# Sending the last 128 row sums as four transposed rows of 128 B instead of within 128 pieces of 64 B

## The chip, the cores and the metric

The kernel runs on one core of a Trainium2 chip. The metric is device time in microseconds (us), lower is better. Every ratio below is between runs in the fast state, on the same chip and in the same rounds. The profile's span, from the first to the last instruction, is some 1.8 us shorter than the device time of the same run; small differences are read best from the profiles. Two limits: each profile is one execution, and profiles of different experiments come from different chips; and the four runs that issue many stores one by one were executed once, so their state is unknown.

Engines: VectorE (DVE in the profile), ScalarE (ACT), SyncE (SP, whose queue "SPq" issues nearly all transfers), and 16 DMA engines that move the data.

## The reference

```python
batch, seq, dim = 32, 512, 1024
# x: float32, (batch, seq, dim); multiplier: 0.5
def reference(x, multiplier):
    return (np.sum(x, axis=-1) * multiplier).astype(np.float32)
```

That is 16,384 rows of 1024 floats (67.1 MB) in, and 16,384 sums (64 KB) out.

## The kernel before

Each of the 128 partitions owns rows that lie next to each other in memory, and takes them in blocks of 16. Seven blocks come from the first 14,336 rows, the eighth from the last 2,048. VectorE sums whole blocks; from the middle of the seventh block on, VectorE and ScalarE share the rows, and those of the eighth arrive in ever smaller pieces, so that little work is left when the last byte is in. The very last piece is columns 576 to 1023 of one row per partition.

```python
x_rows = x_flat[0 : P * own, :].rearrange("(p c) d -> p c d", p=P)
x_last = x_flat[P * own : N, :].rearrange("(p c) d -> p c d", p=P)
out_rows = out_flat[0 : P * own].rearrange("(p c) -> p c", p=P)
out_last = out_flat[P * own : N].rearrange("(p c) -> p c", p=P)
...
for lo, hi in [(0, 8), (8, 13), (13, 15)]:               # rows of the last block
    loads.append(nc.sync.dma_start(out=t[:, lo:hi, :], in_=x_last[:, lo:hi, :]))
for lo, hi in ((0, cut), (cut, D)):                      # cut = 576: the last row in two
    loads.append(nc.sync.dma_start(out=t[:, B - 1, lo:hi], in_=x_last[:, B - 1, lo:hi]))
early = nc.sync.dma_start(out=out_rows, in_=res[:, 0:own])      # 56 KB of results
for r in range(B - 1):
    ...                                                  # ScalarE or VectorE, a row each
dve_span(t, B - 1, 0, cut, part)
final = dve_span(t, B - 1, cut, D, res[:, rows - 1 : rows], start=part)
seen = nop_after(nc.sync, loads[-8:] + acts[-1:], [])
store = nc.sync.dma_start(out=out_last, in_=res[:, own:])       # 8 KB, 64 B a partition
nop_after(nc.sync, [early, final], [store])
```

`out_last` gives each partition 16 neighbouring results, so the last store is 128 pieces of 64 B, and it must wait for the very last sum.

Of the kernel before, what the change touches and what calls it, by code (L numbers as in the profile page):

```python
# [1 line left out]

# [4 lines left out]


@with_exitstack
def kernel(  # L10
    ctx: ExitStack,
    tc: tile.TileContext,
    x: bass.AP,
    multiplier: float,
    out: bass.AP,
):










    nc = tc.nc
    P = nc.NUM_PARTITIONS
    fp32 = mybir.dt.float32
    ADD = mybir.AluOpType.add  # L30

    x_flat = x.flatten_outer_dims()
    N, D = x_flat.shape
    rows = N // P
    out_flat = out.rearrange("b s -> (b s)")
    mul = float(multiplier)

    B = 16
    n_blocks = rows // B
    assert N == P * rows and rows == n_blocks * B  # L40
    own = rows - B
    x_rows = x_flat[0 : P * own, :].rearrange("(p c) d -> p c d", p=P)
    x_last = x_flat[P * own : N, :].rearrange("(p c) d -> p c d", p=P)
    out_rows = out_flat[0 : P * own].rearrange("(p c) -> p c", p=P)
    out_last = out_flat[P * own : N].rearrange("(p c) -> p c", p=P)

    x_pool = ctx.enter_context(tc.tile_pool(name="x", bufs=3))
    res_pool = ctx.enter_context(tc.tile_pool(name="res", bufs=1))
    sums = res_pool.tile([P, rows], fp32, name="sums")
    res = res_pool.tile([P, rows], fp32, name="res")  # L50
    part = res_pool.tile([P, 1], fp32, name="part")

    SYNC = mybir.DependencyInfo(mybir.DependencyClass.Sync, mybir.DependencyReason.DATA)
    ORDER = mybir.DependencyInfo(
        mybir.DependencyClass.NoSync, mybir.DependencyReason.SCHED_ONLY
    )

    def nop_after(engine, waits_for, follows):
        i = engine.nop()
        for w in waits_for:  # L60
            tc.add_manual_dep(i.ins, w.ins.name, SYNC, reason="end seen here")
        for f in follows:
            tc.add_manual_dep(i.ins, f.ins.name, ORDER, reason="in this order")
        return i

    loads = []
    acts = []

    def act_row(t, r, col):
        acts.append(nc.scalar.activation(  # L70
            out=t[:, r, :],
            in_=t[:, r, :],
            func=mybir.ActivationFunctionType.Copy,
            scale=mul,
            accum_out=res[:, col : col + 1],
        ))

    def dve_span(t, r, lo, hi, dst, start=0.0):
        mid = (lo + hi) // 2
        return nc.vector.tensor_tensor_reduce(  # L80
            out=t[:, r, lo:mid],
            in0=t[:, r, lo:mid],
            in1=t[:, r, mid:hi],
            scale=mul,
            scalar=start,
            op0=ADD,
            op1=ADD,
            accum_out=dst,
        )

    for b in range(n_blocks - 1):
        c0 = b * B
        t = x_pool.tile([P, B, D], fp32, name="xb")
        loads.append(nc.sync.dma_start(out=t, in_=x_rows[:, c0 : c0 + B, :]))  # L94
        h = B if b < n_blocks - 2 else B // 2
        nc.vector.reduce_sum(  # L96
            out=sums[:, c0 : c0 + h], in_=t[:, 0:h, :], axis=mybir.AxisListType.X
        )
        nc.vector.tensor_single_scalar(  # L99
            out=res[:, c0 : c0 + h],  # L100
            in_=sums[:, c0 : c0 + h],
            scalar=mul,
            op=mybir.AluOpType.mult,
        )
        for r in range(h, B):
            act_row(t, r, c0 + r)

    c0 = (n_blocks - 1) * B
    t = x_pool.tile([P, B, D], fp32, name="xb")
    cut = 576  # L110
    pieces = [(0, 8), (8, 13), (13, 15)]
    for lo, hi in pieces:
        loads.append(
            nc.sync.dma_start(  # L114
                out=t[:, lo:hi, :], in_=x_last[:, lo:hi, :]
            )
        )
    for lo, hi in ((0, cut), (cut, D)):
        loads.append(
            nc.sync.dma_start(  # L120
                out=t[:, B - 1, lo:hi], in_=x_last[:, B - 1, lo:hi]
            )
        )
    early = nc.sync.dma_start(out=out_rows, in_=res[:, 0:own])
    on_act = {4, 5, 6, 7, 11, 12, 14}
    for r in range(B - 1):
        if r in on_act:
            act_row(t, r, c0 + r)
        else:
            dve_span(t, r, 0, D, res[:, c0 + r : c0 + r + 1])  # L130
    dve_span(t, B - 1, 0, cut, part)
    final = dve_span(t, B - 1, cut, D, res[:, rows - 1 : rows], start=part)




    seen = nop_after(nc.sync, loads[-8:] + acts[-1:], [])
    store = nc.sync.dma_start(out=out_last, in_=res[:, own:])
    tc.add_manual_dep(store.ins, seen.ins.name, ORDER, reason="in this order")
    for a in acts[-len(on_act) :]:  # L140
        tc.declare_no_dep(store.ins, a.ins.name, reason="waited for by the nop in front")
    nop_after(nc.sync, [early, final], [store])

    def start_loads_at_entry(nc_):



        entry, *rest = nc_.main_func.blocks
        is_sp = lambda i: i.engine == mybir.EngineType.SP
        is_load = lambda i: type(i).__name__ == "InstDMACopy"  # L150
        for block in rest:
            body = list(block.instructions)
            own = [i for i in body if is_sp(i)]
            if not any(is_load(i) for i in own):
                continue
            lead = []
            for i in own:
                if not is_load(i) or i.sync_info.on_wait:
                    break
                lead.append(i)  # L160
            names = {i.name for i in lead}
            block.instructions = [i for i in body if i.name not in names]
            head = list(entry.instructions)
            at = next(
                k for k, i in enumerate(head) if is_sp(i) and type(i).__name__ == "InstDrain"
            )
            entry.instructions = head[:at] + lead + head[at:]
            return

    nc.at_finalize(start_loads_at_entry)  # L170


# [1 line left out]
_INS = ['x', 'multiplier']  # L174
_OUTS = [((32, 512), 'float32')]

_NUMBERS = {'multiplier': 0.5}


# [26 lines left out]
```

## Time and profile before

| | before |
|---|---|
| device time, median (lowest to highest) | 162.13 us (162.12 to 162.49) |
| span in the profile | 160.517 us |
| busy share of the DMA engines | 97.5% |
| VectorE / ScalarE busy | 119.3 us / 17.3 us |
| last accumulator out | 158.315 us |
| last store: issue; last count of its semaphore | 158.344 us; 159.765 us |

The loads fill the DMA engines until the last one has landed at 157.72; then come the last sum and the last store. I call the last 2.20 us, from the last sum's accumulator to the end of the span (160.517 - 158.315), the **tail**; it doesn't contain the small differences in when the loads end. The prediction shows its lines.

How to read a store here: the profile's bar "DMA_DIRECT2D" on SPq is the issue alone. The bytes move later, in packets on the DMA engines, and the store has landed only when every engine has counted the semaphore up. I give three times for a store, all from the start of its bar: the length of the **bar**, the start of its **first packet**, and its **last count**. The first is a line of the profile, the other two are from the trace's packet and semaphore records. ("Descriptors" in the prediction are the orders for the single pieces.)

### The profile page before, as it was taken

Reading aid. Unit: us, or ns where it says so; the run is one execution under the profiler, and the core shown is the slowest. Engines: PE = TensorE matmul, PEld = TensorE weight load, DVE = VectorE, ACT = ScalarE, POOL = GpSimd, SP = SyncE. Lnnn points to the kernel's source line nnn. Section 1 sums busy time; section 2 is a strip of 40 time slices with the busy share of each in tenths; the row PEclk is TensorE's granted clock in tenths of the full one; section 3 lists DMA queues with packets and bytes.
Section 4 is the critical chain, followed back from the end, with each engine's and each line's share of the span. In section 5 each row is a group of like instructions: output and inputs, shape, how many; then the busy total and the mean of one; then the engine's idle time right before and its main releaser. Section 6 shows DMA issues by size and latency. Waiting matters only on the chain.

```text
span 160.5 us, 138 instructions
## 1 busy us (share of the span) xinstructions
DVE 119.3 (74%) x34; ACT 17.3 (11%) x31; POOL 0.2 (0%) x4
## 2 busy tenths in 40 slices
DVE  0000059998699968999599995999959999597443
ACT  0000000000000000000000000000000000599952
POOL 0000000000000000000000000000000000000000
DMA  8996996996996996996996997997998998999991
GB/s 261 523 523 261 523 506 278 523 490 294 523 490 294 523 490 294 523 490 294 523 490 294 523 474 310 523 441 343 523 425 359 523 425 359 392 433 425 439 368 50
DMA packets 2016, 67.18 MB, mean 418 GB/s; under 512 B 480, under 2 KB 608, under 8 KB 736
## 3 DMA queue, kind: packets, MB, share of 16 engines
q1 hardware_dynamic: 2016, 67.18, 97.5%
HBM read 67.11 MB, written 0.07 MB: 418 GB/s over the span
## 4 chain that ended last, share of the span: by engine, by line
DMA 75%; DVE 22%; SPq 1%; issue 0%; DVEq 0%
DMA xb<-in_x_dram 75%; DVE sums L96 21%; SPq L114 1%; DVE xb L80 0%; SPq L120 0%; SPq L94 0%; DVE res L99 0%; DVEq L80 0%; DVEq L201 0%
## 5 line engine op out<-in xcount | busy, mean ns | idle before, releaser
L96 DVE TENSOR_REDUCE sums<-xb 128x16 f32<-128x16384 f32 (+1 forms) x7 | 112.0, 16001 | 33.6 <-DMA xb<-in_x_dram 33.6
L70 ACT ACT_TABLE_LOAD x1 | 1.3, 1283 | 138.2 <-DMA xb<-in_x_dram 138.2
L70 ACT ACTIVATE xb<-xb 128x1024 f32<-128x1024 f32 x15 | 15.7, 1045 | 2.1 <-DMA xb<-in_x_dram 2.1
L80 DVE CUSTOM_DVE_ANT_0 xb<-xb 128x512 f32<-128x512 f32 (+1 forms) x9 | 5.6, 663 | 5.0 <-DMA xb<-in_x_dram 5.0
L70 ACT ACTIVATION_READ_ACCUMULATOR xb<-xb 128x1 f32 x15 | 2.8, 187 | 0.0
L99 DVE TENSOR_SCALAR res<-sums 128x16 f32<-128x16 f32 (+1 forms) x7 | 1.2, 174 | 0.2
L80 DVE DVE_READ_ACCUMULATOR2_ANT res<- 128x1 f32 x9 | 0.7, 83 | 0.0
L80 DVE CUSTOM_DVE_ANT_0 xb<-xb,part 128x224 f32<-128x224 f32 x1 | 0.5, 452 | 0.2 <-DMA xb<-in_x_dram 0.2
L187 POOL MEMSET const-bfloat16-1.0<- 128x1 bf16 x1 | 0.1, 102 | 0.0
L187 POOL MEMSET const-uint8-127<- 128x1 uint8 x1 | 0.1, 102 | 0.0
L187 POOL MEMSET const-float32-0.0<- 128x1 f32 x1 | 0.1, 99 | 0.2 <-issue 0.2
L187 POOL MEMSET const-float32-1.0<- 128x1 f32 x1 | 0.1, 99 | 0.0
L80 DVE DVE_READ_ACCUMULATOR2_ANT part<- 128x1 f32 x1 | 0.1, 83 | 0.0
## 6 DMA issues: line engine op xcount, KB each, us to landing
xb<-in_x_dram SPq DMA_DIRECT2D x1, 4096.0 KB, 31.1
xb<-in_x_dram SPq DMA_DIRECT2D x1, 2560.0 KB, 36.9
xb<-in_x_dram SPq DMA_DIRECT2D x1, 1024.0 KB, 38.9
xb<-in_x_dram SPq DMA_DIRECT2D x1, 288.0 KB, 39.1
xb<-in_x_dram SPq DMA_DIRECT2D x1, 224.0 KB, 39.2
xb<-in_x_dram SPq DMA_DIRECT2D x7, 40.8
out_dram<-res SPq DMA_DIRECT2D x1, 56.0 KB, 10.0
out_dram<-res SPq DMA_DIRECT2D x1, 8.0 KB, 1.4
```

Of the source, the lines that this page charges most:

```text
L70: acts.append(nc.scalar.activation(out=t[:, r, :], in_=t[:, r, :], func=mybir.ActivationFunctionType.Copy, scale=mul, accum_out=res[:, col ...
L80: return nc.vector.tensor_tensor_reduce(out=t[:, r, lo:mid], in0=t[:, r, lo:mid], in1=t[:, r, mid:hi], scale=mul, scalar=start, op0=ADD, o ...
L96: nc.vector.reduce_sum(out=sums[:, c0 : c0 + h], in_=t[:, 0:h, :], axis=mybir.AxisListType.X)
L99: nc.vector.tensor_single_scalar(out=res[:, c0 : c0 + h], in_=sums[:, c0 : c0 + h], scalar=mul, op=mybir.AluOpType.mult,)
L114: nc.sync.dma_start(out=t[:, lo:hi, :], in_=x_last[:, lo:hi, :])
L187: nc = _bacc.Bacc("TRN2", target_bir_lowering=False, num_devices=1)
```

## The change

The intent is to have less at the end: rather than 128 pieces of 64 B, only four rows of 128 B should be stored after the last sum. To that end the last row of all partitions becomes the last 128 rows of x, so that its sums are 512 neighbouring bytes of the output. They are a column, one per partition. VectorE's transpose in 32x32 squares turns it into four rows, on partitions 0, 32, 64 and 96. The other 15 results of each partition leave a little earlier, from ScalarE's queue.

```diff
+    few = B - 1
+    x_next = x_flat[P * own : P * (own + few), :].rearrange("(p c) d -> p c d", p=P)
+    x_last = x_flat[P * (own + few) : N, :]
+    out_next = out_flat[P * own : P * (own + few)].rearrange("(p c) -> p c", p=P)
+    S = 32
+    out_last = out_flat[P * (own + few) : N].rearrange("(q s) -> q s", s=S)
...
+    last = res_pool.tile([P, S], fp32, name="last")
+    turned = res_pool.tile([P, S], fp32, name="turned")
+    nc.vector.memset(last, 0.0)
...
-    final = dve_span(t, B - 1, cut, D, res[:, rows - 1 : rows], start=part)
+    dve_span(t, B - 1, cut, D, last[:, 0:1], start=part)
+    final = nc.vector.transpose(out=turned, in_=last)
+    middle = nc.scalar.dma_start(out=out_next, in_=res[:, own:])
...
-    store = nc.sync.dma_start(out=out_last, in_=res[:, own:])
+    store = nc.sync.dma_start(out=out_last, in_=turned[0:P:S, :])
```

(Cut here: the loads of the last block read `x_next` and `x_last` accordingly, `res` has one column less, and the wait at the end includes `middle`.)

More of the change, by code (lines that the diff above doesn't have):

```diff
@@ L42 @@
     x_rows = x_flat[0 : P * own, :].rearrange("(p c) d -> p c d", p=P)
-    x_last = x_flat[P * own : N, :].rearrange("(p c) d -> p c d", p=P)
+    few = B - 1
+    x_next = x_flat[P * own : P * (own + few), :].rearrange("(p c) d -> p c d", p=P)
+    x_last = x_flat[P * (own + few) : N, :]
     out_rows = out_flat[0 : P * own].rearrange("(p c) -> p c", p=P)
-    out_last = out_flat[P * own : N].rearrange("(p c) -> p c", p=P)
+    out_next = out_flat[P * own : P * (own + few)].rearrange("(p c) -> p c", p=P)
+    S = 32
+    out_last = out_flat[P * (own + few) : N].rearrange("(q s) -> q s", s=S)
     x_pool = ctx.enter_context(tc.tile_pool(name="x", bufs=3))
@@ L49 @@
     sums = res_pool.tile([P, rows], fp32, name="sums")
-    res = res_pool.tile([P, rows], fp32, name="res")
+    res = res_pool.tile([P, own + few], fp32, name="res")
+    last = res_pool.tile([P, S], fp32, name="last")
+    turned = res_pool.tile([P, S], fp32, name="turned")
+    nc.vector.memset(last, 0.0)
     part = res_pool.tile([P, 1], fp32, name="part")
@@ L114 @@
             nc.sync.dma_start(
-                out=t[:, lo:hi, :], in_=x_last[:, lo:hi, :]
+                out=t[:, lo:hi, :], in_=x_next[:, lo:hi, :]
             )
@@ L120 @@
             nc.sync.dma_start(
-                out=t[:, B - 1, lo:hi], in_=x_last[:, B - 1, lo:hi]
+                out=t[:, B - 1, lo:hi], in_=x_last[:, lo:hi]
             )
@@ L131 @@
     dve_span(t, B - 1, 0, cut, part)
-    final = dve_span(t, B - 1, cut, D, res[:, rows - 1 : rows], start=part)
+    dve_span(t, B - 1, cut, D, last[:, 0:1], start=part)
+    final = nc.vector.transpose(out=turned, in_=last)
+    middle = nc.scalar.dma_start(out=out_next, in_=res[:, own:])
     seen = nop_after(nc.sync, loads[-8:] + acts[-1:], [])
-    store = nc.sync.dma_start(out=out_last, in_=res[:, own:])
+    store = nc.sync.dma_start(out=out_last, in_=turned[0:P:S, :])
     tc.add_manual_dep(store.ins, seen.ins.name, ORDER, reason="in this order")
-    for a in acts[-len(on_act) :]:
-        tc.declare_no_dep(store.ins, a.ins.name, reason="waited for by the nop in front")
-    nop_after(nc.sync, [early, final], [store])
+    nop_after(nc.sync, [early, middle, final], [store])
     def start_loads_at_entry(nc_):
```

## The prediction

> **What bounds the kernel now.** I began with the page's engine table and its chain of work that ended last, to learn whether an engine or the transfers set the end.
>
> ```profile
> span 160.5 us, 138 instructions
> DVE 119.3 (74%) x34; ACT 17.3 (11%) x31; POOL 0.2 (0%) x4
> ...
> q1 hardware_dynamic: 2016, 67.18, 97.5%
> ...
> DMA 75%; DVE 22%; SPq 1%; issue 0%; DVEq 0%
> ```
>
> The 16 DMA engines are busy 97.5% of the span. VectorE is 74% busy, and its 22% of the chain is an alternative path, not a second bound: the chain in order of time hops from a load to a reduction and on to the next load only because a buffer is freed there, while other loads keep the queue full. 67.11 MB in about 157.7 us is 426 GB/s: loading is the floor, and the change loads the same bytes. What it can change is the end. So next the timeline from 157.5 us:
>
> ```profile
> 157.41 0.19 ACT L70 ACTIVATION_READ_ACCUMULATOR xb<-xb 128x1 f32 x1
> 157.57 0.08 DVE L80 DVE_READ_ACCUMULATOR2_ANT part<- 128x1 f32 x1
> 157.85 0.45 DVE L80 CUSTOM_DVE_ANT_0 xb<-xb,part 128x224 f32<-128x224 f32 x1 [0.20 <-DMA xb<-in_x_dram]
> 158.23 0.08 DVE L80 DVE_READ_ACCUMULATOR2_ANT res<- 128x1 f32 x1
> 158.34 0.34 SPq L138 DMA_DIRECT2D out_dram<-res  x1
> ```
>
> The last load (448 columns of the last row of every partition) lands at about 157.7; VectorE sums it from 157.85, its accumulator is out at 158.31, the last store is issued at 158.34. ScalarE has been done since 157.60 (157.41 + 0.19). The DMA issues, and the DMA view of 158 to 160.5 us, show what follows:
>
> ```profile
> out_dram<-res SPq DMA_DIRECT2D x1, 56.0 KB, 10.0
> out_dram<-res SPq DMA_DIRECT2D x1, 8.0 KB, 1.4
> ```
>
> ```profile
> DMA packets 144, 0.01 MB, mean 3 GB/s; under 512 B 144, under 2 KB 144, under 8 KB 144
> ```
>
> The 8 KB store takes 1.4 us from issue to landing. Its 144 packets are 128 of 64 B and 16 of 4 B, one per engine, which count the semaphore up. The trace's packet records place all of them between 159.24 and 159.46:
>
> ```profile
> 158.34:159.24 0.90, 0.00 (x0) 0.00 (x0) 0.00 (x0) 1.00 0.04 3
> 159.24:159.46 0.22, 0.00 (x0) 0.00 (x0) 0.00 (x0) 1.00 0.28 23
> 159.46:160.52 1.06, 0.00 (x0) 0.00 (x0) 0.00 (x0) 1.00 0.00 0
> ```
>
> (stretch, length, busy time of DVE, ACT and POOL, clock, DMA share, GB/s). So the tail after the last sum is: 0.03 to the issue; 0.90 from issue to the first packet; 0.22 of packets; then about 0.31 from the last packet to the last semaphore count (159.76 in the trace's semaphore records; the 16 counts arrive one by one, 11.7 ns apart, over 0.18 us); then 0.75 of drains and barriers to 160.52. Only the 0.22, and perhaps part of the 0.90, depend on how the output is cut into pieces.
>
> **What the Trainium skill says.** "DMA: Bandwidth & Descriptors", section "Why a DMA increments its semaphore by 16 and not by 1": a transfer is spread over the largest k up to 16 that divides the slowest dimension on both sides, and the sequencer writes the missing 16 - k counts at once. The trace agrees for 128 partitions: 16 counts, one per engine. The new store, 4 rows of 128 B, would therefore use 4 engines; nothing in the trace before shows that yet. Same page, "Specifications": under 512 B the DMA engine does a read-modify-write. Before, 64 B pieces fall under it, and after, 128 B pieces still do; the change cuts their number from 128 to 4, not their kind. In the trace a 64 B packet takes 8 to 11 ns and 8 of them on one engine about 55 ns, so there is little cost to cut. "Perfetto Trace Analysis", section "DMA Instruction — HWDGE (DVE, Sync)": the data movement is outside the issue's bar, and the final count waits for the confirmed write. The trace agrees: a bar of 0.34 us, a landing after 1.4. "VectorE: DVE Perf Modes", section "The three transpose paths": VectorE transposes 32x32 blocks only, 128x128 bf16 in 311 ns. No transpose is in the trace before.
>
> **The change, part by part.**
> 1. *Removed:* the 8 KB store of 128 x 64 B on the last path. In its place a store of 4 x 128 B. Packets: 8 per engine become 1, which saves about 7 of 8 times 55 ns, 0.05 us. Engines: their starts are spread over about 0.15 us with 16 engines (the packet span of 0.22 less 0.055 and the 4-byte packet); with 4 engines at 11.7 ns from one to the next the last starts 0.035 us after the first, so 0.14 us less. Together about -0.19 us. The 0.90 from issue to first packet may also hold some descriptor making that shrinks from 128 to 4 pieces. But the 56 KB store (448 B pieces) and the 8 KB store have almost the same issue bar, 0.35 and 0.34, with the same number of pieces, so the trace cannot tell how it goes with their number. I allow 0 to 0.2 and count -0.05. The confirmation, 0.3 us, stays.
> 2. *Added on the path:* one transpose, 128x32 fp32, between the last sum and the store; the order of instructions shows it last on VectorE, waiting for VectorE's own semaphore. Its time: the 128x16 multiply by a scalar took 174 ns and the 128x8 one 171[...]. From the skill's 311 ns for 128 columns, less 96 columns at one cycle of 0.96 GHz (100 ns), I get 0.21 us; this is an estimate. The wait in front: from the end of the last reduction (116.67) to the multiply that waits for it (116.69) the trace has 0.02 us. Then 0.02 to 0.03 from the transpose to the issue, as now. Added: 0.21 + 0.03 = +0.24 us.
> 3. *Added beside the path:* 15 columns of the remaining results leave as a store of 128 x 60 B from ScalarE's queue. ScalarE is done at 157.60, VectorE's last column of these (row 13) at 157.15, so it can be issued at about 157.63. With the same 1.4 us it lands at 159.0 to 159.1; the last store, issued at about 158.58 (158.34 + 0.24), lands around 159.8. It has some 0.7 us to spare.
> 4. *Added at the start:* a memset of 128x32 on VectorE, which waits for the first load for 22 us anyway: 0.
> 5. *Moved:* the rows of the last two stretches of x. The pieces of 8, 5 and 2 rows start 60 KB apart from partition to partition instead of 64; the pieces of the last row are now 128 neighbouring rows, 4 KB apart instead of 64. Descriptor sizes stay: 32 KB, 20 KB, 8 KB, 2304 B, 1792 B. In the trace, 32 KB packets take about 1.213 us (27.0 GB/s an engine), 2304 B about 93 ns (24.8), 1792 B about 74 ns (24.2): each engine runs near one rate with a few ns added per packet, so addresses are not what limits it, and I count 0.
> 6. *Same:* the 56 KB store stays in its place behind the loads in SyncE's queue, landing at about 157.97, ahead of the end; the barrier at the end stays.
>
> Sum: +0.24 - 0.19 - 0.05 = 0.00, with about 0.15 either way. The time before is a median of 162.13. I put 0.02 on top for a second queue whose end must be waited for, and predict **162.15 us**.
>
> **The rivals.**
> (a) *Small writes are dearer than the packets show.* If the receipt of many part-line writes or making 128 descriptors is most of the 0.90 + 0.31, then 4 pieces gain up to half of it. Against: the first 4 B packet of an engine and its count are 0.29 us apart, the last 0.31, though the first did not wait for anyone; so the queue of 64 B writes adds almost nothing. For: the 0.90 is not broken up in the trace. It would make 161.7 to 161.9.
> (b) *The transpose is all that is felt.* If the packet span is hidden behind the same fixed times and the store lands 1.4 us after issue as before, the loss is the full +0.24, and a 4-byte-wide transpose that takes two passes would add 0.05 to 0.1: 162.4 to 162.5. For: a fixed cost dominates the 1.4.
> (c) *The middle store takes the place of the wait.* It has 0.7 us to spare; a first transfer on ScalarE's queue would have to be twice as slow as SyncE's. SyncE's first load has its first packet 1.08 us after the span's start, no worse than the 0.90 of the last store, so a first use costs little there. If it did happen: 162.5 to 163.
> (d) *The addresses change the load rate.* The last 8 MB take about 20 us of the span; 1% more or less over them is 0.2 us, and a real conflict among 128 neighbouring rows would touch only 512 KB, 1.2 us of transfer: even half again as slow it costs 0.6. Against: the packet rates in point 5. It would make 161.9 or up to 162.7.
>
> **Range and chances.** The sum's own uncertainty is 0.15, (a) and (b) pull 0.25 to 0.35 to either side, and the three runs before scatter from 162.12 to 162.49 by themselves. So the range is **161.85 to 162.5**. A 2% change would be 3.24 us; the whole tail from the last sum to the end of the span is 2.2 us, of which over 1.6 are fixed times that stay. No rival reaches 2%: **faster 0.01, same 0.98, slower 0.01**.
>
> **What would show it.** In the profile after: the loads' chain ends at about 157.7 as before; a transpose of 0.2 us after the last accumulator; the last store issued near 158.6, 0.24 later than now; its landing in about 1.2 us instead of 1.4; 4 packets of 128 B and 4 counts in the place of 128 and 16; the middle store issued by ScalarE near 157.6 and landed by 159.2; a span of 160.4 to 160.7. I would be wrong if the last store lands in under 1.0 us (rival a) or still takes 1.4 (b), if what the final wait ends on is the middle store (c), or if the last load lands away from 157.7 by more than 0.2 us (d).

Its times from the packet records need a correction: all are 0.06 us too late. The packets of the store before begin at 159.18, not at 159.24: the first packet is 0.84 us after the issue, the last one 1.04, the last count 1.42. The window from 158.34 to 159.24 that I quoted shows it, with a DMA share of 0.04 that should have been 0. So the 0.90 is 0.84, the 0.31 from the last packet to the last count is 0.37, the 0.29 in rival (a) is 0.35, and the 1.08 in (c) is 1.01. The sum is not touched by this. The 0.96 GHz in point 2 also comes out of the trace before: a reduction of 16,384 columns takes 17,220 ns and one of 8,192 takes 8,687, which is 1.04 ns a column.

## The result

| | before | after |
|---|---|---|
| device time, median (lowest to highest), 6 runs each | 162.12 us (162.11 to 162.49) | 162.53 us (162.45 to 162.76) |
| ratio | | 1.0024 (95% interval 1.0011 to 1.0037) |
| span in the profile | 160.517 us | 160.971 us |
| tail: last accumulator to the end of the span | 2.202 us | 2.646 us |

A ratio is the mean time of one kernel's runs over the mean of the other's in the same rounds, so it is not quite the ratio of the medians. By the 2% rule this is "same", as predicted; but it is about 0.4 us slower, clear of noise, and just above the predicted range (162.5).

First the page of the kernel after: the transfers by queue, and the two new VectorE instructions (count, busy us, mean ns; then idle time in front and its cause).

```profile
q1 hardware_dynamic: 1880, 67.17, 97.0%
q10 hardware_dynamic: 144, 0.01, 0.1%
...
L58 DVE MEMSET last<- 128x32 f32 x1 | 0.1, 85 | 1.8 <-PEq L194 1.8
...
L141 DVE STREAM_TRANSPOSE turned<-last 128x32 f32<-128x32 f32 x1 | 0.2, 213 | 0.0
```

The loads are as before. The transpose takes 0.213 us. The second queue is ScalarE's, with its 128 small pieces and 16 counts. Now the chain in order of time, its end (start, length, what):

```profile
118.55 39.17 DMA xb<-in_x_dram
157.72 0.03 issue
157.75 0.02 DVEq L88
157.77 0.09 issue
157.87 0.45 DVE xb L88
158.32 0.02 DVE last L88
158.34 0.02 issue
158.36 0.21 DVE turned L141
```

The last load lands at 157.72 as before, so the new order of the rows costs nothing. The end of the timeline after:

```profile
157.64 0.37 ACTq L142 DMA_DIRECT2D out_dram<-res  x1
157.87 0.45 DVE L88 CUSTOM_DVE_ANT_0 xb<-xb,part 128x224 f32<-128x224 f32 x1 [0.19 <-DMA xb<-in_x_dram]
158.24 0.08 DVE L88 DVE_READ_ACCUMULATOR2_ANT last<- 128x1 f32 x1
158.36 0.21 DVE L141 STREAM_TRANSPOSE turned<-last 128x32 f32<-128x32 f32 x1
158.60 0.63 SPq L147 DMA_DIRECT2D out_dram<-turned  x1
```

The last store is issued at 158.60, where the prediction had it. Its bar is what was not expected: **0.63 us, where the store before had 0.34**, although it has 4 pieces in place of 128. The DMA issues of the kernel after (size, us to landing) show that the middle store is no obstacle: it lands 1.5 us after 157.64.

```profile
out_dram<-res SPq DMA_DIRECT2D x1, 56.0 KB, 10.0
out_dram<-res ACTq DMA_DIRECT2D x1, 7.5 KB, 1.5
```

From the trace's packet and semaphore records, the last store of both kernels:

```
us from the start of the issue   bar     first packet   last packet   last count
before: 128 pieces of 64 B       0.343   0.837          1.041         1.421
after:    4 pieces of 128 B      0.630   1.227          1.293         1.620
```

The packets themselves are quicker, 0.07 us from first to last where it was 0.20. But the first comes 0.39 us later. This delay and the 0.245 us that the transpose adds before the issue, less 0.19 saved after the first packet, are the whole loss of 0.44. The rest of the tail, from the last count to the end, is 0.752 us in both.

### The profile page after: what moved, and what is told of

Its sections match the earlier page's. It is cut to its first block, busy times and chain, and to the rows that moved or that the text cites. A ratio compares the mean times of both kernels' runs of the same rounds, so it can differ in the third digit from the quotient of the medians.

```text
span 161.0 us, 142 instructions
## 1 busy us (share of the span) xinstructions
DVE 119.6 (74%) x36; ACT 17.3 (11%) x31; POOL 0.2 (0%) x4
## 4 chain that ended last, share of the span: by engine, by line
DMA 75%; DVE 22%; SPq 1%; issue 0%; DVEq 0%
DMA xb<-in_x_dram 75%; DVE sums L104 21%; SPq L122 1%; DVE xb L88 0%; SPq L128 0%; SPq L102 0%; DVE turned L141 0%; DVE res L107 0%; DVEq L88 0%; DVE last L88 0%
```

## The experiments

After the result I had these theories for the longer issue:

- **A**: a store on fewer than 16 engines is dearer to issue, because the issuing engine writes the missing counts.
- **B**: the store from ScalarE's queue a moment earlier gets in the way.
- **C**: the new order of the rows costs (the chain above already spoke against it).
- **D**: the transpose is hidden, and the whole loss is the store's.
- **E**: a store whose rows lie partitions apart (0, 32, 64, 96) is slow to issue.
- **F**: the first store of this kind is slow, later ones are not.

In the edits below "..." marks lines that are cut.

### Without the transpose, as a column

```diff
-    final = nc.vector.transpose(out=turned, in_=last)
...
-    store = nc.sync.dma_start(out=out_last, in_=turned[0:P:S, :])
+    store = nc.sync.dma_start(out=out_col, in_=last[:, 0:1])    # 128 pieces of 4 B
```

> The changed kernel without the transpose, the last 128 sums leaving as 128 pieces of 4 B from one column (16 engines). Theory A (a store on 4 engines is dearer to issue): issue bar back at 0.34 us, first packet 0.84 us after the issue, landing 1.42 us after it, issue at 158.36, so the time of the kernel before, 162.1 to 162.2. Theory B (the ScalarE store a moment earlier, or the second queue as such, slows SyncE's issue and the end): the bar stays near 0.63 and the time stays at 162.3 or more. Theory C (the new order of the rows costs): time above 162.3 with the last load later than 157.75.

Measured: 167.66 us (167.54 to 167.95), right result, 1.0342 times the kernel before. No theory had this. The bar was 0.344 us, which speaks against B: the ScalarE store stood in front of it just the same. But the DMA issues of this run show what came after:

```profile
out_dram<-last SPq DMA_DIRECT2D x1, 0.5 KB, 7.3
```

512 B took 7.3 us to land. As a test of the time this run failed; I return to it below.

### With the transpose, as a column

```diff
     final = nc.vector.transpose(out=turned, in_=last)
-    seen = nop_after(nc.sync, loads[-8:] + acts[-1:], [])
+    seen = nop_after(nc.sync, loads[-8:] + acts[-1:] + [final], [])
-    store = nc.sync.dma_start(out=out_last, in_=turned[0:P:S, :])
+    store = nc.sync.dma_start(out=out_col, in_=last[:, 0:1])
```

> The changed kernel with the transpose kept and waited for, but the sums leaving as 128 pieces of 4 B as in the run before. Theory A: the transpose alone, +0.25 us on that run: issue at 158.60, bar 0.34, landing after 1.42; time 162.35 to 162.45. Theory D (the transpose is hidden, the whole loss is the 4-piece store): 162.1 to 162.2.

Measured: 168.1 us, right result. The absolute time suffers from the same slow store. Its tail is 8.357 us against 8.074 in the run before it, 0.28 us more, and from accumulator to issue it is 0.320 against 0.028: the transpose and its waits are on the path and not hidden (theory D falls).

### The four rows without the transpose

```diff
-    final = nc.vector.transpose(out=turned, in_=last)
...
-    store = nc.sync.dma_start(out=out_last, in_=turned[0:P:S, :])
+    store = nc.sync.dma_start(out=out_last, in_=last[0:P:S, :])   # wrong result on purpose
```

> Wrong result on purpose: four rows of 128 B are stored straight from the untransposed tile. Theory A: issue at 158.36, bar 0.63, landing 1.62 us after the issue: +0.20 on the kernel before, 162.30 to 162.40. If the 4-piece store cost nothing by itself and only followed the transpose badly: bar 0.34 and 162.1.

Measured: 162.32 us (162.26 to 162.39), ratio 1.0010 (0.9998 to 1.0023); the result is wrong. The timeline of this run has the long bar without any transpose in front:

```profile
158.13 0.08 DVE L88 DVE_READ_ACCUMULATOR2_ANT last<- 128x1 f32 x1
158.24 0.64 SPq L146 DMA_DIRECT2D out_dram<-last  x1
```

The last count came 1.619 us after the issue, and the tail was 2.400. So by the profiles the four-row store costs 0.20 us by itself (2.400 - 2.202), and the transpose about 0.25 (2.646 - 2.400), which agrees with the 0.245 read from accumulator to issue. The ratio alone would not show the 0.20: its interval touches 1.

### Stores of different shapes, one by one

The kernel before, with part of its results held back and stored at the end in thirteen stores, each of which waits for the one in front to land.

```diff
-    early = nc.sync.dma_start(out=out_rows, in_=res[:, 0:own])
+    early = nc.sync.dma_start(out=out_rows[:, 32:own], in_=res[:, 32:own])
...
+    def alone(lo, hi, step):      # waits for the store in front, then stores 128 B a row
+        ...
+        i = nc.sync.dma_start(out=out_rows[lo:hi:step, 0:32], in_=res[lo:hi:step, 0:32])
+    alone(13, 29, 1); alone(0, 128, 32); alone(1, 5, 1); alone(5, 13, 1); ...
```

> The kernel before with 32 of its early columns kept back and stored at the end in thirteen stores, one after the other on an idle queue, 128 B a piece: 16, 4 (32 partitions apart), 4 (side by side), 8, 2, 1, 31, 16, 15, 16, 4, 8 and 3 pieces. Theory A, by engines: 16 pieces have a bar of about 0.34 us, every count that uses fewer than 16 engines about 0.6 us, whether side by side or apart; if the missing counts are written one by one the bar grows with 16 minus k (0.34 + 0.024 times the missing ones: 8 pieces 0.53, 4 pieces 0.63, 1 piece 0.70), if at once it is 0.63 for all. Theory E (partitions apart are slow): 4 apart 0.63, 4 side by side 0.34. Theory F (a first use of a shape is slow, a repeat is not): the second 4 and 8 pieces at 0.34.

Measured, right result; the first six, and the repeats (us from the start of each issue):

```
pieces of 128 B               engines   bar     first packet   last count
16 side by side               16        0.345   0.850          1.344
 4, 32 partitions apart        4        0.638   1.232          1.634
 4 side by side                4        0.278   0.748          1.143
 8 side by side                8        0.276   0.755          1.160
 2 side by side                2        0.235   0.724          1.062
 1                             1        0.227   0.715          1.049
...
 4 side by side, later         4        0.253   0.740          1.142
 8 side by side, later         8        0.276   0.761          1.151
```

Theory A falls: fewer engines are not slower but quicker. Only one store has a long bar, the one with its rows 32 partitions apart. But it was also the first on fewer than 16 engines, so E and F are both left.

### Is it the first use?

The early store in two parts, of 8 and of 120 partitions, so that SyncE has issued stores on 8 and on 15 engines before the last one.

```diff
-    early = nc.sync.dma_start(out=out_rows, in_=res[:, 0:own])
+    early = nc.sync.dma_start(out=out_rows[0:8, :], in_=res[0:8, 0:own])
+    early_b = nc.sync.dma_start(out=out_rows[8:P, :], in_=res[8:P, 0:own])
...
```

> The changed kernel, right result, with one edit: the 56 KB early store goes out as two, of 8 and of 120 partitions, so that SyncE has issued stores on 8 and on 15 engines some 10 us before the last one. Theory F (the first store on fewer than 16 engines is slow to issue, later ones are quick): the last store's bar falls from 0.63 to 0.28 us and it lands 1.14 us after its issue instead of 1.62; time 162.53 - 0.48 = 162.05, within 0.1. Theory E (rows 32 partitions apart are slow to issue): bar 0.63, landing 1.62, time 162.5 as the change itself.

Measured: 162.64 us (162.54 to 162.67), right result, ratio 1.0027 (1.0015 to 1.0040). The view of the store's line:

```profile
L148 SPq DMA_DIRECT2D out_dram<-turned x1: 607/607/607, 158.4 to 158.4; - x1
```

The bar is still 0.607 us and the last count comes after 1.632. The same edit without the transpose. Its output is wrong, which doesn't matter for the time.

> Wrong result on purpose: as the run before, without the transpose (rows of the untransposed tile are stored). Theory F: 0.25 us less than that run: 161.8; what the 4-piece store is worth by itself when it isn't the first, 162.13 - 0.28 = 161.85. Theory E: 162.3 as in the run without the transpose before.

Measured: 162.33 us, ratio 1.0009 (0.9996 to 1.0022), bar 0.610. Both runs show what E expected. F falls for a first store on fewer than 16 engines; whether only the first store of rows that lie apart is slow, the next run tests.

A further run of single stores had the order of shapes changed and small packed pieces added:

```diff
...
+    rows_again(0, 8, 1); rows_again(0, 128, 32); rows_again(0, 128, 32); rows_again(0, 4, 1)
+    rows_again(0, 128, 8); rows_again(0, 16, 1)
+    packed(1)                              # 128 pieces of 4 B, one behind the other in memory
+    alone(out_rows[:, 0:1], res[:, 0:1])   # 128 pieces of 4 B, 448 B apart
+    packed(2); packed(4); packed(8); packed(16)
```

> The kernel before with thirteen stores of results that are already there, one after the other, at its end. Order: 8 pieces of 128 B side by side, 4 pieces 32 partitions apart, the same again, 4 side by side, 16 pieces 8 partitions apart, 16 side by side; then 128 pieces of 4 B packed in memory, 128 of 4 B 448 B apart, packed pieces of 8, 16, 32 and 64 B; then the right values of all rows. Theory F: the first (8 pieces) has the bar of 0.63 and all later ones about 0.28, also 32 partitions apart. Theory E: the first 0.28, both stores 32 partitions apart 0.63. Of the small pieces: if writes to one stretch of memory from different engines hold each other up, the packed 4 B land after some 7 us, the 4 B pieces 448 B apart after 1.4, and the packed ones get quicker up to 64 B at 1.42; if 4 B is slow by itself, both 4 B stores take 7 us.

```
                                       bar     first packet   last count
  8 of 128 B side by side              0.352   0.779          1.179
  4 of 128 B, 32 partitions apart      0.605   1.233          1.642
  the same again                       0.510   1.149          1.536
  4 of 128 B side by side              0.262   0.735          1.133
 16 of 128 B, 8 partitions apart       0.541   1.194          1.687
 16 of 128 B side by side              0.330   0.814          1.303
128 of   4 B, packed in memory         0.361   0.859          7.926
128 of   4 B, 448 B apart              0.350   0.840          1.425
128 of   8 B, packed                   0.333   0.825          3.078
128 of  16 B, packed                   0.332   0.824          1.844
128 of  32 B, packed                   0.332   0.831          1.400
128 of  64 B, packed                   0.332   0.829          1.397
```

Two things follow. **First**, a repeat saves some 0.1 us of the slow form and no more; and 16 rows 8 partitions apart, on all 16 engines, are slow in the same way, so it is neither the number of engines nor the missing counts. **Second**, the slow landing of the column runs is traced to its layout: 4 B pieces are not slow as such (1.425 us when they are 448 B apart), but packed against each other in memory they are, and the cost falls as the pieces grow and is gone at 32 B. The issue and the start of the packets are as usual in those stores; the wait is between the packets and the counts. What makes it is not shown.

### Sixteen rows side by side in place of four

```diff
-    store = nc.sync.dma_start(out=out_last, in_=turned[0:P:S, :])
+    store = nc.sync.dma_start(out=out_last, in_=turned[0:16, 0 : P // 16])  # wrong on purpose
```

(`out_last` is cut into 16 rows of 8 results accordingly.)

> Wrong result on purpose: the changed kernel with the last store as 16 pieces of 32 B from 16 partitions, on all 16 engines. Theory F and theory E agree: bar 0.34, landing 1.34, and with the transpose in front 162.13 + 0.25 - 0.08 = 162.3. If small neighbouring pieces are what is slow (4 B pieces took 7.3 us to land), the landing is later than 1.5.

Measured: 162.31 us (162.25 to 162.33), ratio 1.0007 (0.9992 to 1.0022). Bar 0.357, last count 1.326 us after the issue, tail 2.358: the transpose, less what fewer packets save. As both theories expected, this run does not tell E from F. It does show that a store after the transpose and from the transposed tile can be quick.

### The four rows side by side

The decisive test of E in its place: the same bytes, pieces, engines and place in memory, only from partitions 0 to 3.

```diff
-    store = nc.sync.dma_start(out=out_last, in_=turned[0:P:S, :])
+    store = nc.sync.dma_start(out=out_last, in_=turned[0 : P // S, :])      # wrong on purpose
```

> Wrong result on purpose: the changed kernel with its last store taking partitions 0 to 3 of the transposed tile instead of 0, 32, 64 and 96; pieces, bytes, engines and the place in memory are the same. Theory E (a store whose rows lie partitions apart is slow to issue): bar about 0.28 us, first packet about 0.75 after the issue, landing 1.14; the span 0.48 shorter than the changed kernel's and the time 162.05 to 162.15, that of the kernel before. Theory G (a small store on few engines is slow at this place for some other reason): bar 0.63, landing 1.62, time 162.5.

Measured: 162.17 us (162.12 to 162.39), ratio 1.0005 (0.9991 to 1.0019). The end of the timeline of this run:

```profile
158.38 0.21 DVE L141 STREAM_TRANSPOSE turned<-last 128x32 f32<-128x32 f32 x1
158.62 0.34 SPq L147 DMA_DIRECT2D out_dram<-turned  x1
```

With the transpose still in the path, and ScalarE's store too, the bar is 0.343 us, the last count comes after 1.159, and the tail is 2.191 where the change has 2.646. The step over partitions is what costs, 0.46 us in this place (2.646 - 2.191); theory G falls.

### Mended with four stores of one row

```diff
+    for q, engine in enumerate((nc.sync, nc.scalar, nc.sync, nc.scalar)):
+        stores.append(engine.dma_start(
+            out=out_last[q : q + 1, :], in_=turned[q * S : q * S + 1, :]))
...
+    nop_after(nc.sync, [early, middle, final] + stores[1::2], [stores[2]])
```

> A mended version, right result: the four rows leave as four stores of one partition each, two from SyncE's queue and two from ScalarE's, so that no store steps over partitions. Theory E: bars of about 0.23 us on SyncE, the second issued about 0.3 after the first, landing 1.06 after its issue, so 1.35 after the first issue instead of 1.62: 162.25 to 162.3, quicker than the changed kernel but not than the one before. If issues of two queues hold each other up, 162.5.

Measured: 162.85 us (162.82 to 162.99), right result, ratio 1.0046 (1.0034 to 1.0059): slower than the change itself, a miss. SyncE's second issue followed 0.355 us after its first, ScalarE's second 0.518 after its first, whose bar was 0.487, beside SyncE's first issue, where the second had 0.233. So the last count came 1.610 us after the first issue, no earlier than that of the single store (1.620), where I had expected 1.35. Then the end grew: from the last count to the end of the span it is 0.981 us instead of 0.752, because SyncE went through more waits, one after the other, before the final barrier: from the last count to its first step of that barrier 0.308 us instead of 0.079. The saving was eaten by more issues and more waits.

### Which steps are slow

Twelve single stores once more, one look:

```diff
...
+    rows_again(0, 4, 1); rows_again(0, 8, 2); rows_again(0, 16, 4); rows_again(0, 64, 16)
+    alone(out_rows[0:128:32, 0:32], res[0:4, 0:32])     # apart in memory only
+    alone(out_rows[0:4, 0:32], res[0:128:32, 0:32])     # apart on the partitions only
+    ...
```

> The kernel before with twelve stores one after the other at its end: 4 pieces of 128 B side by side, then 2, 4 and 16 partitions apart, 4 with only the memory rows 32 apart, 4 with only the partitions 32 apart, the same into one packed stretch, 4 side by side from partition 30, 64 pieces 2 apart, 64 side by side, 4 side by side, then the right values of all rows. Theory E1 (any step over partitions on the SBUF side is slow): side by side bars of 0.26 to 0.28 and landing at 1.14 also where memory steps; all others 0.5 to 0.64 and 1.53 to 1.64. E2 (only far steps, over more than some partitions): 2 and 4 apart like side by side. E3 (the memory side's step counts as well): the fifth slow too.

```
pieces of 128 B                                  bar     first packet   last count
 4 side by side                                  0.332   0.757          1.149
 4,  2 partitions apart                          0.722   1.355          1.757
 4,  4 apart                                     0.622   1.257          1.655
 4, 16 apart                                     0.528   1.164          1.575
 4, side by side, 32 rows apart in memory        0.268   0.742          1.134
 4, 32 partitions apart, side by side in memory  0.542   1.183          1.575
 4, 32 partitions apart, packed in memory        0.510   1.151          1.536
 4 side by side, from partition 30               0.257   0.746          1.130
64, 2 apart                                      0.526   1.173          1.715
64 side by side                                  0.495   1.149          1.688
```

(The table leaves out the second "4 side by side": 0.258, 0.738, 1.133.) Two of these bars in the timeline of this run, the first store side by side and the one 2 partitions apart:

```profile
159.82 0.33 SPq L149 DMA_DIRECT2D out_dram<-res  x1
```

```profile
161.03 0.72 SPq L149 DMA_DIRECT2D out_dram<-res  x1
```

E1 holds for the step: every step over partitions that was tried is slow, even one of 2, while the step in memory, of 32 rows, costs nothing (E2 and E3 fall). Crossing from partition 31 to 32 costs nothing either (the row "from partition 30"). Which step is slowest is not shown: the bars of the first three stepped stores fall in the order of their issue, 0.722, 0.622, 0.528, and a repeat of one and the same store had been 0.1 us quicker. But one line contradicts "all side by side are quick": 64 rows side by side. A last look was for that (the same edit with other rows, not printed).

> Settles one loose end: 64 pieces side by side had a bar of 0.495 us and landed after 1.69, as slow as rows that lie apart, though they don't step. The kernel before with twelve stores one after the other at its end, all side by side from partition 0, 128 B a piece: 4, 64, 64, 32, 32, 24, 48, 96, 112, 120, 128 pieces, then the right values of all rows. If 64 was slow only because it came right after a stepped store, both 64s are quick here (0.33, 1.42). If several partitions to one engine are slow unless it is 8 of them, then 64, 32, 24, 48, 96 and 112 are slow (0.5 to 0.7) and 120 and 128 quick (0.33 to 0.35). If only 64 is odd, the rest is quick.

```
side by side     bar     last count
 64              0.526   1.718
 64 again        0.466   1.660
 32              0.329   1.322
 24              0.308   1.253
 48              0.315   1.374
 96              0.316   1.393
112              0.316   1.386
120              0.335   1.372
128              0.356   1.446
```

(Left out: 4 pieces, 0.332 and 1.150, and 32 again, 0.321 and 1.331.) Only 64 is odd, and it is slow in a run without any stepped store. Why the step, and why just 64 of these counts, takes the slow way is not to be seen in these runs; I leave it open. The change does not store 64 rows, so its explanation doesn't need it.

## Why the prediction was wrong

The path was read rightly, and all terms but one were right to 0.05 us. By the profiled runs, as differences of the tail:

| term of the prediction's sum | predicted, us | measured, us |
|---|---|---|
| transpose and its waits, accumulator to issue | +0.24 | +0.245 (0.274 - 0.029) |
| fewer packets, fewer engines one after the other | -0.19 | -0.14 (0.066 - 0.204) |
| last packet to last count ("stays") | 0.00 | -0.05 (0.327 - 0.380) |
| issue to first packet | -0.05 | **+0.39** (1.227 - 0.837) |
| a second queue to wait for at the end | +0.02 | 0.00 (0.752 us in both) |
| sum | +0.02 | **+0.44** (2.646 - 2.202) |

- **The step that failed** is in part 1: "The 0.90 from issue to first packet may also hold some descriptor making that shrinks from 128 to 4 pieces ... I allow 0 to 0.2 and count -0.05". I took a store's issue time for a matter of how many pieces it has, and allowed no loss. The trace before couldn't contradict this, as all its transfers run over all 128 partitions. The new store steps 32 partitions from row to row, and such a store's bar is 0.63 us and its first packet 0.39 us later. Of the 0.39, 0.29 lie in the bar and 0.10 between the bar and the first packet. The number of pieces does help, as I had thought: four rows side by side have their first packet after 0.74 to 0.76 and land after 1.13 to 1.15 on an idle queue, where the 128 pieces need 1.42; in place of the last store the first packet comes after 0.768, which is 0.07 sooner, near the 0.05 that I counted. With the rows side by side the tail is 2.191, and my forecast would have held (162.17).
- **Luck.** The -0.19 for the packets was 0.05 too much, and the confirmation that should have stayed became 0.05 shorter; the two misses cancel. The 0.21 us for the transpose of float32 came from a figure for bf16; it met the 0.213 measured, but only this one size was run.
- **Rivals.** (a) had the wrong sign in this store; the gain it hoped for exists only without the step. (b) came nearest with its 162.4 to 162.5, but for a wrong reason: the store did not take 1.4 us as before, it took 1.62, and the transpose was not dearer. (c) did not happen: ScalarE's store had its last count 1.468 us after 157.643, which is 159.11, more than 1 us before the last store's. (d) did not happen: the last load landed at 157.72.
- **Points 3 to 6** held: a hidden memset of 85 ns, a second queue that costs nothing here, and unchanged loads.
- **The range** was too narrow for what it rested on. No store of this shape was in the trace, and I still gave the store's issue no way to get slower.
- **The chances** came out right. But that nothing in the tail could reach 2% was not safe: the same 512 bytes as a column made the kernel 3.4% slower.

No version beat the kernel before. The best form of the idea, with the rows side by side, would only tie: it pays 0.25 us for the transpose and gains 0.26 from the quicker store (1.421 - 1.159). And this transpose leaves the rows 32 partitions apart (the run that took partitions 0 to 3 had a wrong result), so that form isn't to be had with it alone.

## What to carry to other kernels

Count the tail of a kernel by its terms, accumulator to issue, issue to first packet, packets, last count, and check that the trace holds an example of each new transfer's shape before its term is called known. Take the rows of a store on the last path from neighbouring partitions: here a step over partitions cost more than 124 saved pieces gave back. And don't pack very small pieces from many partitions against each other in memory: 128 pieces of 4 B took 6.5 us longer to land than the same pieces spread out or 32 B pieces in a row.

## What the Trainium skill lacked or had wrong

- "DMA: Bandwidth & Descriptors" gives for an SBUF-side access pattern a rule on steps over partitions in the later dimensions only; that a step in the leading dimension is slow is on no page I read. Measured: 4 rows of 128 B side by side have a bar of 0.25 to 0.34 us and land after 1.13 to 1.16; 2, 4, 16 or 32 partitions apart 0.51 to 0.72 and 1.54 to 1.76. A step of 32 rows on the memory side costs nothing (0.268, 1.134).
- The same page doesn't have the oddity of 64 partitions: 0.466 to 0.526 us and 1.66 to 1.72, where 48 and 96 have 0.32 and 1.37 to 1.39.
- Its section "Why a DMA increments its semaphore by 16 and not by 1" was right for k = 4 (k engines move the transfer): the trace shows five counts, one 1.01 us after the issue, before the first packet (1.227) and so not by an engine that moved data, and four after it. That writing the missing counts is not what makes the store slow is shown by 4 rows side by side, with the same k, and by 16 rows 8 apart with no missing count (bar 0.541).
- Its section "Specifications" has one threshold, 512 B, under which the DMA engine does a read-modify-write; no run here shows one as such. Below it the runs show a further distinction that this page doesn't make: packed 4, 8, 16, 32 B pieces land after 7.93, 3.08, 1.84, 1.40 us, but 4 B pieces 448 B apart after 1.425.
- "VectorE: DVE Perf Modes", section "The three transpose paths": its 311 ns for 128 columns gave me an estimate of 0.21 us for 32; the trace has 0.213. The page doesn't say what a store of the result costs: the rows wanted here lie 32 partitions apart.
- "Perfetto Trace Analysis", section "DMA Instruction — HWDGE (DVE, Sync)", puts descriptor making inside the bar and the movement outside. The runs agree in part: a bar longer by 0.29 us went with a first packet later by 0.39, so that 0.10 of the delay lies after the bar.
